# Second score matmul of the forgetting and stick-breaking heads over 128 rows, with zero rows in a low tile per head

## The chip, the cores and the metric

The kernel runs on one core of one Trainium2 chip. The metric is the device time of one execution in microseconds (us). Times of the kernel before come from three timed runs and from one further execution that the hardware profiler recorded. In the profile PE is TensorE (matmuls), PEld its weight loads, DVE is VectorE, ACT is ScalarE, POOL is GpSimd and SP is SyncE, which issues most DMAs. L65 is line 65 of the kernel.

## The reference

The program is a trunk of two layers on 512 tokens of width 1024. In each layer one input projection feeds three causal mixers of eight heads with 64 dimensions each; their outputs are projected, gated, added and projected again:

```python
h = rms_norm(x, g_norm) * (1.0 + scale) + shift
z = h @ w_in                                    # queries, keys, values, gates
y_fox = fox_attention(fq, fk, fv, log_f)        # softmax(q k^T / 8 + F_i - F_j), causal
y_dsa = dsa_attention(q_d, dk, dv, iq, ik, iw)  # one shared key head, top-k by indexer scores
y_sb = stick_breaking_attention(sq, sk, sv)     # sigmoid(z) * prod(1 - sigmoid(z)) of later keys
mixed = m_fox * (y_fox @ w_br_fox) + m_dsa * (y_dsa @ w_br_dsa) + m_sb * (y_sb @ w_br_sb)
x = x + gate * (mixed @ w_out)
```

The output is `rms_norm(x, g_final)` after the second layer. What matters here are the scores `q k^T` of the forgetting (fox) and the stick-breaking (sb) heads, 16 heads per layer, computed per block of 128 queries against all keys up to that block: 128, 256, 384 and 512 keys.

## The kernel before

**Precision by splitting.** Matmul operands are rounded to a short type, so each operand x is kept as a high part (`hi`, L116, a copy by ACT into the short type) and a low part (`lo`, L119, x minus high, by DVE). A projection adds three products, high by high, high by low and low by high (`mm3`): 24 matmuls for 8 chunks of 128 rows.

**Scores.** A head has 64 dimensions and the array contracts over 128 rows. So a head's query tile (`stack_q`, L440) holds the query's high part in one half of its rows and its low part in the other; for an even head the high part is in rows 0 to 63, for an odd one in rows 64 to 127. The key's high tile `kh` (`pair_k`, L766) holds the key's high part twice, in both halves. The first score matmul of a block, over 128 rows, so gives (query high + query low) by key high. The second adds query high by key low: it takes only the 64 rows in which the query's high part lies (`q[hr, c]`, where `hr(o)` is the half of head o) and the same rows of the key's low tile `kl`. One `kl` serves the two heads of a pair, one in each half. Both matmuls go into the same PSUM bank, with the same 128 query columns as weights (L637, L638 for fox; L656, L657 for sb).

The DSA heads have one key for all heads. Their `stack_k` (L447) makes a `kh` and a `kl` of 128 rows from a tile that holds the key twice, and both of their score matmuls contract over 128 rows (L641).

**What follows a score block.** Fox and DSA: DVE adds the bias and takes the row's minimum (L623), ACT exponentiates (L624). In a fox block POOL has first broadcast the forget row and masked it (L632, L634). Sb: ACT writes two sigmoids (L660, L661), POOL masks both (L662, L663), DVE does a running product (L665) and a multiplication (L666). Then PE transposes the probabilities, ACT and DVE split them (L117, L121), and PE multiplies them with the values.

**Buffers.** Tiles come from pools by tag. The tag `kh` has five buffers, `kl` three, `qst` (query tiles) six; in `project` (L808) the mixed activations reuse them, the first five chunks `kh`, the others `kl`. The four small PSUM banks `pt` hold scores and transposes.

**Order.** The order on PE and on SP is written out by hand when the program is built: one stream of projections (GEMMs), into which timed threads (heads, indexer, modulation) put their blocks. The clock of this order (`mm`, L63) counts the columns of each matmul at 2400 per us, whatever its rows. A head becomes startable 3.0 us of that clock after its pair's key projection (`pair`), heads start every 15 (fox), 13 (sb) and 14 us (DSA), and a small bank counts as held for 4.0 us. The order on ACT, DVE and POOL is chosen by the framework's planner from its own estimates; each engine then runs its queue in that order. The modulation of later layers (`ada`) runs on DVE beside all this, and so does, once the indexer's scores are complete, its top-k (L613, L614).

Of the kernel before, what the change touches and what calls it, by code (L numbers as in the profile page):

```python
# [12 lines left out]
F32 = mybir.dt.float32  # L13
F32R = mybir.dt.float32r
# [4 lines left out]
P = 128  # L19
D = 1024  # L20
S = 512
# [16 lines left out]
class Trunk:  # L38
# [12 lines left out]

# [1 line left out]
    def t(self, shape, dt, tag, bufs=1):  # L53
# [7 lines left out]

# [1 line left out]
    def mm(self, o, s, m, first, last):  # L63
# [26 lines left out]
    def bank(self, us):  # L90
        """Wait for one of the four small banks, to be held for about us."""
        if min(self.tfree) > self.now:
            yield lambda: min(self.tfree) <= self.now
        self.tfree[self.tfree.index(min(self.tfree))] = self.now + us
# [19 lines left out]

# [1 line left out]
    def hi(self, out, in_, scale=1.0):  # L116
# [35 lines left out]
    def gemm_b(self, ps, ws, n, tbs, ks=range(KC)):  # L152
        """h[tb] @ w for up to two token blocks: n <= 256 columns each, in one bank."""
        for i, tb in enumerate(tbs):
            sl = slice(tb * P, tb * P + P)
            o = ps[:, i * n:(i + 1) * n]
            for k in ks:
                wh, wl = ws[k // 4]
                hh, hl = self.hH[:, k, sl], self.hL[:, k, sl]
                self.mm(o, hh, wh[:, k % 4, :], k == 0 and i == 0, False)  # L160
                self.mm(o, hh, wl[:, k % 4, :], False, False)
                self.mm(o, hl, wh[:, k % 4, :], False, k == KC - 1)
                yield
# [33 lines left out]

# [1 line left out]
    def setup(self):  # L199
# [73 lines left out]

# [1 line left out]
    def ada_sum(self, acc, v, j, k, k0=0):  # L275
# [35 lines left out]
    def ada_first(self, b):  # L311
        """Columns 256b.. of scale and shift; the first rows of shift are left to the tensor engine."""
        n = PE_ROWS[b]
        tag = "tmp" if b % 2 else "fm"
        accs = [self.t([P, 256], F32, tag, 2) if part or n < 4 else None for part in range(2)]
        vs = []
        for j in range(KC // 2):
            for part in (1, 0):
                v = self.t([P, 2, 256], F32, *(("pt", 4) if b % 2 and not part else ("y", 8)))
                src = self.a["w_ada"][0, j * 256:(j + 1) * 256, part * D + b * 256:part * D + b * 256 + 256]  # L320
                self.nc.sync.dma_start(v, src.rearrange("(k p) n -> p k n", p=P))
                if not part and j < n:
                    vs.append(v)
                    continue
                for i in range(2):
                    self.ada_sum(accs[part], v, i, 2 * j + i, 0 if part else 2 * n)
        return accs, vs
# [22 lines left out]

# [1 line left out]
    def rstd(self, out, ssq, n):  # L352
# [47 lines left out]
    def rows(self, r, tag, tbs):  # L400
        """rstd of token blocks tbs along the free dimension, on every partition."""
        rb = self.ps(tag)
        for i, tb in enumerate(tbs):
            self.tp(rb[:, i * P:(i + 1) * P], r[:, tb:tb + 1].to_broadcast([P, P]))
        return rb
# [22 lines left out]

# [1 line left out]
    def rope(self, outs, x, cb, sb):  # L430
# [15 lines left out]

    def stack_k(self, src, tags=(("kh", 5), ("kl", 3))):  # L447
        pt = self.ps("t")
        for tb in range(NB):
            self.tp(pt[:, tb * P:(tb + 1) * P], src[:, tb, :])  # L450
        kh, kl = [self.t([P, S], F32R, *x) for x in tags]
        self.hi(kh, pt)
        self.lo(kl, pt, kh)
        return kh, kl

# [1 line left out]
    def small_raw(self, l, j):  # L457
# [86 lines left out]

# [1 line left out]
    def rope_bank(self, ps, tbs, qs, off, scale, key):  # L546
# [27 lines left out]

# [1 line left out]
    def indexer(self, l, iqs):  # L576
# [40 lines left out]

# [1 line left out]
    def softmax_block(self, ps, bias, n, b, den):  # L619
# [6 lines left out]

    def fox_block(self, h, b, q, kh, kl, hr, den):
        nc = self.nc
        n = (b + 1) * P
        part = 32 * (h % 4)  # L630
        fm = self.t([P, 512], F32, "fm", 2)
        nc.gpsimd.partition_broadcast(fm[:, :n], self.frow[h // 4][part:part + 1, :n])  # L632
        d = fm[:, b * P:n]
        nc.gpsimd.affine_select(d, d, [[-1, P]], ALU.is_ge, BIG, base=0, channel_multiplier=1)  # L634
        ps = self.ps("t")
        c = slice(b * P, n)
        self.mm(ps[:, :n], q[:, c], kh[:, :n], True, False)  # L637
        self.mm(ps[:, :n], q[hr, c], kl[hr, :n], False, True)  # L638
        return self.softmax_block(ps, fm[:, :n], n, b, den[:, b:b + 1])
# [10 lines left out]

    def sb_block(self, b, q, kh, kl, hr):
        nc = self.nc
        n = (b + 1) * P
        c = slice(b * P, n)
        ps = self.ps("t")
        self.mm(ps[:, :n], q[:, c], kh[:, :n], True, False)  # L656
        self.mm(ps[:, :n], q[hr, c], kl[hr, :n], False, True)  # L657
        u = self.t([P, 512], F32, "fm", 2)
        s = self.t([P, n], F32, f"pr{b}", 1 + (b != 1))
        nc.scalar.activation(u[:, :n], ps[:, :n], AF.Sigmoid, scale=-1.0)  # L660
        nc.scalar.activation(s, ps[:, :n], AF.Sigmoid)  # L661
        nc.gpsimd.affine_select(u[:, c], u[:, c], [[-1, P]], ALU.is_ge, 1.0, base=-1, channel_multiplier=1)  # L662
        nc.gpsimd.affine_select(s[:, c], s[:, c], [[-1, P]], ALU.is_ge, 0.0, base=-1, channel_multiplier=1)  # L663
        rev = u[:, :n][:, ::-1]
        nc.vector.tensor_tensor_scan(rev, rev, rev, 1.0, ALU.mult, ALU.bypass)  # L665
        nc.vector.tensor_tensor(s[:, :n - 1], s[:, :n - 1], u[:, 1:n], ALU.mult)  # L666
        return s
# [78 lines left out]

# [1 line left out]
    def values(self, l, col, u, out, key):  # L748
# [17 lines left out]
    def pair_k(self, ps, k):  # L766
        kl = self.t([P, S], F32R, "kl", 3)
        for o in range(2):
            a = slice(64 * o, 64 * o + 64)
            b = slice(64 - 64 * o, 128 - 64 * o)  # L770
            kh = self.t([P, S], F32R, "kh", 5)
            self.hi(kh[a, :], ps[a, :])
            self.hi(kh[b, :], ps[a, :])
            self.lo(kl[a, :], ps[a, :], kh[a, :])
            k.append(kh)
        k.append(kl)

    def pair(self, l, kind, cols, p, scale, st):
        """Query and key stacks and gate of heads 2p and 2p + 1."""
        q, k = st[p] = ([], [])  # L780
        yield from self.a_gemm(l, cols[0] + p * P, lambda ps: self.pair_q(ps, scale, q))
        yield from self.a_gemm(l, cols[1] + p * P, lambda ps: self.pair_k(ps, k))
        self.mark((kind, l, "pair", p), 3.0)
# [24 lines left out]
    def project(self, l, gate, out, st):  # L808
        nc = self.nc
        last = l + 1 == DEPTH  # L810
        mH, mL = [], []
        for m in range(KC):
            mH.append(self.t([P, S], F32R, *(("kh", 5) if m < 5 else ("kl", 3))))
            mL.append(self.t([P, S], F32R, *(("qst", 6) if m < 6 else ("pt", 4))))
            self.hi(mH[m], self.mix[m])
            self.lo(mL[m], self.mix[m], mH[m])
# [61 lines left out]

# [1 line left out]
    def opening_first(self, xc, rb, mod, fox, h, sps, sms, post):  # L880
        """The opening of layer 0, on two chunks of h at a time, as scale and shift come."""
        whole = slice(0, S)
# [73 lines left out]
    def opening(self, l, fox, st, gs, xc, mod):  # L956
        """Small columns and the first pair, on the parts of h as they come."""
        q, k = st[0] = ([], [])
# [38 lines left out]
    def attention(self, l, L):  # L997
        """Starts the heads of the three branches at an even pace."""
        hr = lambda o: slice(64 * o, 64 * o + 64)
        self.av_busy = False  # L1000
        prev = None
        self.spawn(self.indexer(l, L["iq"]))
        for kind, scale, period in (("fox", -0.125, FOX_T), ("sb", 0.125, SB_T), ("dsa", -0.125, DSA_T)):
            st, gs, ys = L[kind]
            den = y = None
            for h in range(NH):
# [13 lines left out]
                if kind == "fox":  # L1020
                    block = lambda b, h=h, q=q, k=k, o=o, d=den[:, o, :]: self.fox_block(h, b, q, k[o], k[2], hr(o), d)
                elif kind == "sb":
                    block = lambda b, q=q, k=k, o=o: self.sb_block(b, q, k[o], k[2], hr(o))
                else:
                    block = lambda b, q=q, d=den[:, o, :]: self.dsa_block(b, q, d)
# [176 lines left out]
```

## Time and profile before

| | us |
|---|---|
| median of three runs | 1333.29 (1332.83 to 1336.71) |
| span of the profiled execution, first to last instruction | 1328.5 |
| median of the runs less the profiled span | 4.8 |
| PE busy | 1297.9 |
| PEld busy | 1086.6 |
| DVE busy | 972.8 |
| ACT busy | 667.6 |
| POOL busy | 136.1 |

The profiled execution's own time is known as its span; the 4.8 us are the difference to the runs' median. Matmuls are pipelined, so the durations of neighbours overlap: a 128x512 matmul is shown as some 0.39 us long while the next one starts 0.23 us after it. What a matmul costs PE is therefore read from start to start. The granted clock of TensorE was 0.993 over the whole span, and 1.00 in all stages used below. Moving operands are written as partitions x columns, and `64*128` is the part of the array that a matmul uses: 64 rows, 128 columns.

### The profile page before, as it was taken

The numbers are of one execution on the slowest core, as the hardware profiler recorded it, in microseconds if no ns is written. First come the engines' busy times: TensorE is split into PE (matmuls) and PEld (weight loads), VectorE is DVE, ScalarE is ACT, GpSimd is POOL, SyncE is SP. The second block draws the span as 40 slices with busy tenths as digits, with TensorE's granted clock in tenths as the row PEclk, the third lists the DMA queues.
The fourth block names the chain that finished last, engine by engine and source line by source line (L and its number), as shares of the span: only waits on it lengthen the run. The fifth ranks groups of instructions, "written<-read, shape, count | busy, mean of one in ns | idle before, by whom it ended". The sixth has DMA issues, their size and how long they took to land.

```text
span 1328.5 us, 19568 instructions
## 1 busy us (share of the span) xinstructions
PE 1297.9 (98%) x7121; PEld 1086.6 (82%) x7121; DVE 972.8 (73%) x1963; ACT 667.6 (50%) x1303; POOL 136.1 (10%) x311
## 2 busy tenths in 40 slices
PE   6999999999999999999999999999999999999997
PEld 6888777878778888887899987787877888888887
DVE  5788777789999768566567866678989975756553
ACT  4366555464545545453236665556544564554343
POOL 0002122212122000000000212121111100000000
PEclk7999999999999999999999999999999999999999
DMA  9453233332333333242533232223222222324231
GB/s 286 142 175 112 66 110 95 95 91 72 113 92 96 111 94 114 82 133 87 153 100 112 81 96 64 80 64 96 64 80 83 77 80 80 95 64 119 87 103 73
DMA packets 193457, 133.34 MB, mean 100 GB/s; under 512 B 9456, under 2 KB 188224, under 8 KB 193360
## 3 DMA queue, kind: packets, MB, share of 16 engines
q1 hardware_dynamic: 189872, 125.76, 33.1%
q10 hardware_dynamic: 3488, 6.33, 1.5%
q8 instruction: 56, 0.92, 0.3%
q14 instruction: 41, 0.34, 0.1%
HBM read 125.74 MB, written 6.29 MB: 99 GB/s over the span
## 4 chain that ended last, share of the span: by engine, by line
PE 88%; DVE 4%; DMA 4%; issue 2%; ACT 2%; POOL 0%; SPq 0%; DVEq 0%; POOLq 0%; ACTq 0%
PE pg L65 67%; PE pt L65 10%; PE pt L69 5%; PE pa L65 5%; DMA y<-in_w_ada_dram 2%; DVE wl L121 1%; DMA raw<-in_w_in_dram 1%; DMA vs<-in_x_dram 1%; DVE fm L665 0%; DMA raw<-in_w_ada_dram 0%; ACT wh L117 0%; DMA y<-in_w_kv_up_dram 0%; DVE m L613 0%; DVE pr L666 0%; DVE score L614 0%
## 5 line engine op out<-in xcount | busy, mean ns | idle before, releaser
L65 PE MATMUL pg<-hH,wh 128*128 128x512 f32 (+1 forms) x848 | 346.2, 408 | 0.3 <-ACT wh L117 0.3
L65 PE MATMUL pg<-hH,wl 128*128 128x512 f32 (+1 forms) x848 | 331.6, 391 | 0.8 <-DVE wl L121 0.8
L65 PE MATMUL pg<-hL,wh 128*128 128x512 f32 (+1 forms) x848 | 331.2, 391 | 0.0
L121 DVE TENSOR_TENSOR wl<-raw,wh 128x1024 fp32r<-128x1024 f32 (+1 forms) x178 | 217.4, 1222 | 84.3 <-ACT wh L117 81.5
L117 ACT ACTIVATE wh<-raw 128x1024 fp32r<-128x1024 f32 (+1 forms) x178 | 187.8, 1056 | 175.8 <-PE pg L65 113.0
L65 PEld LDWEIGHTS pg<-hH,wh 128*128 128x128 f32 x848 | 159.7, 188 | 37.4 <-issue 8.0
L65 PEld LDWEIGHTS pg<-hH,wl 128*128 128x128 f32 x848 | 159.4, 188 | 37.3 <-DVE wl L121 1.0
L65 PEld LDWEIGHTS pg<-hL,wh 128*128 128x128 f32 x848 | 160.4, 189 | 25.6
L117 ACT ACTIVATE pt<-pt 128x512 fp32r<-128x512 f32 x192 | 83.7, 436 | 109.9 <-PE pt L69 108.0
L65 PE MATMUL pg<-wh,hH 128*128 128x256 f32 x448 | 131.4, 293 | 0.0
L121 DVE TENSOR_TENSOR pt<-pt,pt 128x512 fp32r<-128x512 f32 x192 | 93.3, 486 | 45.7 <-ACT pt L117 44.2
L65 PE MATMUL pg<-wh,hL 128*128 128x256 f32 x448 | 126.5, 282 | 0.0
L65 PE MATMUL pg<-wl,hH 128*128 128x256 f32 x448 | 125.8, 281 | 0.0
L65 PE MATMUL pg<-y,wh 128*128 128x512 f32 x384 | 123.8, 403 | 0.4 <-DVE y L121 0.4
L624 ACT ACTIVATE pr<-pr,nm 128x128 f32<-128x128 f32 (+3 forms) x128 | 71.6, 559 | 80.5 <-DVE nm L623 80.1
L65 PEld LDWEIGHTS pg<-wh,hH 128*128 128x128 f32 x448 | 84.7, 189 | 5.3 <-issue 2.9
L69 PE MATMUL pt<-ident,pr 128*128 128x128 f32 x480 | 84.8, 274 | 1.8 <-DVE pr L666 1.8
L65 PEld LDWEIGHTS pg<-wl,hH 128*128 128x128 f32 x448 | 84.7, 189 | 0.7
L65 PEld LDWEIGHTS pg<-wh,hL 128*128 128x128 f32 x448 | 84.4, 188 | 0.0
L65 PEld LDWEIGHTS pg<-y,wh 128*128 128x128 f32 x384 | 69.0, 188 | 16.9 <-issue 2.3
L65 PE MATMUL pg<-y,wl 128*128 128x512 f32 x192 | 76.0, 396 | 0.0
L69 PEld LDWEIGHTS pt<-ident,pr 128*128 128x128 f32 x480 | 60.1, 141 | 17.3 <-DVE pr L666 2.5
(216 smaller groups left out, 2270.0 us busy)
## 6 DMA issues: line engine op xcount, KB each, us to landing
raw<-in_w_in_dram SPq DMA_DIRECT2D x134, 512.0 KB, 3.9
raw<-in_w_ada_dram SPq DMA_DIRECT2D x32, 512.0 KB, 3.6
raw<-in_w_out_dram SPq DMA_DIRECT2D x16, 512.0 KB, 4.0
y<-in_w_ada_dram SPq DMA_DIRECT2D x24, 256.0 KB, 4.9
raw<-in_w_br_fox_dram SPq DMA_DIRECT2D x8, 512.0 KB, 3.7
raw<-in_w_br_sb_dram SPq DMA_DIRECT2D x8, 512.0 KB, 4.9
raw<-in_w_br_dsa_dram SPq DMA_DIRECT2D x8, 512.0 KB
yf<-xd ACTq DMA_DIRECT2D x16, 256.0 KB, 3.4
```

Source lines behind the costliest of these rows:

```text
L65: self.nc.tensor.matmul(o, s, m, start=first, stop=last, skip_group_check=True)
L69: self.nc.tensor.transpose(o, i, self.ident[:n, :n])
L117: self.nc.scalar.activation(out, in_, AF.Copy, scale=scale)
L121: self.nc.vector.tensor_tensor(out, in_, hi.bitcast(F32), ALU.subtract)
L624: nc.scalar.activation(p, p, AF.Exp, bias=nm, scale=-1.0, accum_out=den)
```

## The change

The second score matmul of a fox or sb block takes all 128 rows of the query tile and of a low tile of its own head. That low tile has the key's low part in the rows where the query's high part lies, and zeros in the other 64 rows, written by a memset on POOL. So there is one `kl` per head instead of one per pair, and the tag `kl` has five buffers instead of three, in all three places that name it. The scratch memory that is kept for dynamic DMAs is set to 2048 bytes per partition. The rest of the diff removes comments and doc strings.

```diff
-    def stack_k(self, src, tags=(("kh", 5), ("kl", 3))):
+    def stack_k(self, src, tags=(("kh", 5), ("kl", 5))):
...
-    def fox_block(self, h, b, q, kh, kl, hr, den):
+    def fox_block(self, h, b, q, kh, kl, den):
...
         self.mm(ps[:, :n], q[:, c], kh[:, :n], True, False)
-        self.mm(ps[:, :n], q[hr, c], kl[hr, :n], False, True)
+        self.mm(ps[:, :n], q[:, c], kl[:, :n], False, True)
...
-    def sb_block(self, b, q, kh, kl, hr):
+    def sb_block(self, b, q, kh, kl):
...
         self.mm(ps[:, :n], q[:, c], kh[:, :n], True, False)
-        self.mm(ps[:, :n], q[hr, c], kl[hr, :n], False, True)
+        self.mm(ps[:, :n], q[:, c], kl[:, :n], False, True)
...
     def pair_k(self, ps, k):
-        kl = self.t([P, S], F32R, "kl", 3)
         for o in range(2):
             a = slice(64 * o, 64 * o + 64)
             b = slice(64 - 64 * o, 128 - 64 * o)
             kh = self.t([P, S], F32R, "kh", 5)
+            kl = self.t([P, S], F32R, "kl", 5)
+            self.nc.gpsimd.memset(kl[b, :].bitcast(F32), 0.0)
             self.hi(kh[a, :], ps[a, :])
             self.hi(kh[b, :], ps[a, :])
             self.lo(kl[a, :], ps[a, :], kh[a, :])
-            k.append(kh)
-        k.append(kl)
+            k.append((kh, kl))
...
-            mH.append(self.t([P, S], F32R, *(("kh", 5) if m < 5 else ("kl", 3))))
+            mH.append(self.t([P, S], F32R, *(("kh", 5) if m < 5 else ("kl", 5))))
...
-    nc = _bacc.Bacc("TRN2", target_bir_lowering=False, num_devices=1)
+    nc = _bacc.Bacc("TRN2", target_bir_lowering=False, num_devices=1, dynamic_dma_scratch_size=2048)
```

In `attention` the two `block` lines pass `*k[o]`, the head's own pair of tiles, in place of `k[o]`, `k[2]` and `hr(o)`.

## Rows read from the trace of the kernel before

**Rows 1.** The page's first part: engine, busy us, share of the span, instructions.

```profile
PE 1297.9 (98%) x7121; PEld 1086.6 (82%) x7121; DVE 972.8 (73%) x1963; ACT 667.6 (50%) x1303; POOL 136.1 (10%) x311
```

**Rows 2.** The page's fourth part, the chain of work that ended last, as shares of the span by engine.

```profile
PE 88%; DVE 4%; DMA 4%; issue 2%; ACT 2%; POOL 0%; SPq 0%; DVEq 0%; POOLq 0%; ACTq 0%
```

**Rows 3.** Busy time by stage. Columns: stretch (us from the span's start), its length, then busy us and number of instructions of PE, PEld, DVE, ACT and POOL, the granted clock of TensorE, the share of the DMA engines, GB/s. The fourth row is from a table of 40 equal slices.

```profile
299.00:432.00 133.00, 131.51 (x692) 105.61 (x691) 126.69 (x240) 65.21 (x128) 26.16 (x55) 1.00 0.32 93
...
731.00:897.00 166.00, 166.00 (x910) 136.82 (x909) 117.50 (x262) 91.44 (x190) 34.87 (x65) 1.00 0.28 77
...
930.00:1063.00 133.00, 132.06 (x690) 106.25 (x689) 121.81 (x223) 65.88 (x130) 19.88 (x52) 1.00 0.27 76
...
398.50:431.70 33.20, 33.20 (x201) 27.73 (x200) 32.32 (x65) 17.75 (x37) 7.75 (x16) 1.00 0.34 96
```

**Rows 4.** Waits of PE from 299 to 432 us: who waited for whom, us in total, times, longest.

```profile
PE pt L69 <- DVE pr L666: 1.1, 1, 1.1
PE pa L65 <- DVE pt L121: 0.4, 1, 0.4
```

**Rows 5.** Busy time by stretch for the instructions that write or read tiles named `kl`: stretch, length, busy us and number of PE, PEld, DVE and ACT, granted clock, DMA. The PE instructions in these stretches are the 64-row score matmuls.

```profile
299.00:432.00 133.00, 10.75 (x26) 4.75 (x26) 3.44 (x5) 0.00 (x0) 1.00 0.32 93
930.00:1063.00 133.00, 10.51 (x26) 4.75 (x26) 4.11 (x6) 0.00 (x0) 1.00 0.27 76
98.00:299.00 201.00, 15.37 (x38) 6.84 (x38) 6.85 (x10) 0.00 (x0) 1.00 0.34 97
731.00:930.00 199.00, 14.73 (x36) 6.58 (x36) 6.17 (x9) 0.00 (x0) 1.00 0.30 80
1063.00:1078.00 15.00, 0.93 (x2) 0.36 (x2) 0.00 (x0) 0.00 (x0) 1.00 0.38 106
```

**Rows 6.** The timeline of PE around eight score blocks: start us, duration us, engine, line, operation, out<-in, rows*columns of the array, moving operand. Four blocks of fox or sb heads (low part with 64 rows) and four of DSA heads (128 rows); in order 512, 512, 384, 384, 256, 256, 128 and 128 columns, the fox or sb block first.

```profile
901.34 0.40 PE L65 MATMUL pt<-kh,qst 128*128 128x512 f32 x1
901.66 0.49 PE L65 MATMUL pt<-kl,qst 64*128 64x512 f32 x1
902.08 0.50 PE L65 MATMUL pg<-hH,wh 128*128 128x512 f32 x1
902.43 0.40 PE L65 MATMUL pg<-hL,wh 128*128 128x512 f32 x1
...
450.00 0.40 PE L65 MATMUL pt<-kh,qst 128*128 128x512 f32 x1
450.23 0.40 PE L65 MATMUL pt<-kl,qst 128*128 128x512 f32 x1
450.47 0.39 PE L65 MATMUL pg<-hH,wh 128*128 128x512 f32 x1
450.70 0.40 PE L65 MATMUL pg<-hL,wh 128*128 128x512 f32 x1
...
301.00 0.33 PE L65 MATMUL pt<-kh,qst 128*128 128x384 f32 x1
...
301.96 0.39 PE L65 MATMUL pg<-hL,wh 128*128 128x512 f32 x1
...
447.92 0.33 PE L65 MATMUL pt<-kh,qst 128*128 128x384 f32 x1
...
448.49 0.39 PE L65 MATMUL pg<-hL,wh 128*128 128x512 f32 x1
...
126.65 0.28 PE L65 MATMUL pt<-kh,qst 128*128 128x256 f32 x1
...
127.51 0.39 PE L65 MATMUL pg<-hL,wh 128*128 128x512 f32 x1
...
445.59 0.28 PE L65 MATMUL pt<-kh,qst 128*128 128x256 f32 x1
...
446.05 0.40 PE L65 MATMUL pg<-hL,wh 128*128 128x512 f32 x1
...
1001.44 0.22 PE L65 MATMUL pt<-kh,qst 128*128 128x128 f32 x1
...
1002.18 0.39 PE L65 MATMUL pg<-hL,wh 128*128 128x512 f32 x1
...
441.56 0.22 PE L65 MATMUL pt<-kh,qst 128*128 128x128 f32 x1
...
442.01 0.40 PE L65 MATMUL pg<-hL,wh 128*128 128x512 f32 x1
```

**Rows 7.** The group of the weight loads of the 64-row matmuls: count | busy us, mean ns of one | idle us of the load port before them, and what ended most of it.

```profile
L65 PEld LDWEIGHTS pt<-kl,qst 64*128 64x128 f32 x128 | 23.4, 183 | 31.1 <-issue 27.9 <-DVE kl L121 0.6 <-DVE mod L290 0.2
```

**Rows 8.** POOL: a memset of 128 columns (count | busy us, mean ns | idle before); the selects of L663 with their shortest, median and longest duration in ns; and two rows of the waits over the whole span (us in total, times, longest).

```profile
L208 POOL MEMSET pen<- 128x128 f32 x1 | 0.2, 206 | 0.0
...
L663 POOL TENSOR_SCALAR_AFFINE_SELECT pr<-pr x64: 289/295/2077, 278.3 to 1068.0; 128x128 f32<-128x128 f32 x64
...
POOL fm L662 <- ACT fm L660: 279.1, 64, 20.2
...
DVE fm L665 <- POOL fm L662: 9.7, 13, 2.4
```

More of the change, by code (lines that the diff above doesn't have):

```diff
@@ L997, in attention @@
     def attention(self, l, L):
-        hr = lambda o: slice(64 * o, 64 * o + 64)
         self.av_busy = False
@@ L1020, in attention @@
                 if kind == "fox":
-                    block = lambda b, h=h, q=q, k=k, o=o, d=den[:, o, :]: self.fox_block(h, b, q, k[o], k[2], hr(o), d)
+                    block = lambda b, h=h, q=q, k=k[o], d=den[:, o, :]: self.fox_block(h, b, q, *k, d)
                 elif kind == "sb":
-                    block = lambda b, q=q, k=k, o=o: self.sb_block(b, q, k[o], k[2], hr(o))
+                    block = lambda b, q=q, k=k[o]: self.sb_block(b, q, *k)
                 else:
```

## The prediction

> **What bounds the kernel now.** I read the page's busy shares first [rows 1]: TensorE (PE) is busy 1297.9 of the 1328.5 us span, 98%, VectorE (DVE) 73%, GpSimd (POOL) 10%. The chain of work that ended last [rows 2] is PE for 88%. So PE's instruction stream sets the time nearly everywhere: what shortens the distance from one matmul's start to the next shortens the kernel, as long as the engines that feed PE keep up. The table of stages [rows 3] shows where that is in doubt. From 299 to 432 us and from 930 to 1063 us, the stick-breaking heads of the two layers, DVE is busy 126.69 and 121.81 of 133 us, beside a PE that is busy 131.51 and 132.06. There two engines are nearly full at once, and what PE gains it can keep only up to DVE's idle time. The waits of PE in the first of these stages [rows 4] are two, 1.1 and 0.4 us, both on DVE: today DVE is just in time.
>
> Then the blocks that the change touches. A score block is two matmuls with the same query tile as weights: with the key's high part (128 rows), then with its low part (64 rows). The same tile query over five stretches [rows 5] counts the 64-row ones: 38, 26, 36, 26 and 2, in all 128 (2 layers, 16 heads, 4 blocks), so 32 of each width, 128, 256, 384 and 512 columns. A mean duration doesn't tell what one costs, since durations overlap; starts in the timeline do. The DSA heads run the same pair of widths with a full 128-row low part, in the same kernel and at the same granted clock, so the price after the change is already in the trace [rows 6].
>
> From the start of the high matmul to the start of the second matmul behind the pair, both followers being 128x512 of a projection:
> - 512 columns: 901.34 to 902.43 with 64 rows, 1.09 us; 450.00 to 450.70 with 128 rows, 0.70 us. Difference 0.39.
> - 384 columns: 301.00 to 301.96, 0.96; 447.92 to 448.49, 0.57. Difference 0.39.
> - 256 columns: 126.65 to 127.51, 0.86; 445.59 to 446.05, 0.46. Difference 0.40.
> - 128 columns: 1001.44 to 1002.18, 0.74; 441.56 to 442.01, 0.45. Difference 0.29.
>
> In the full sequences of 512 columns the loss has three places: the 64-row matmul starts 0.32 us after the high one instead of 0.23, the follower 0.42 after it instead of 0.24, and the matmul after that 0.35 later instead of 0.23. The weight-load row says why: before the 128 loads of 64 rows the load port stood idle 31.1 us, 27.9 of it "issue", waiting for nothing that the profile shows [rows 7]. With full rows a load is done beside the matmul before it; where the row count changes, it is not, on the way in and on the way out.
>
> The Trainium skill (TensorEngine Tiling (Array Packing), Key Properties) says that changing the tiling mode drains TensorE. The trace agrees, with those 0.24 us per load. The same page (Theoretical Speedup) promises up to 2x for contractions of at most 64 rows, by running separate tiles of the array at once. By that rule the change would give up a speed-up instead of removing a cost; the trace shows none of it, since no 64-row matmul here stands beside another one.
>
> **The change part by part.**
> 1. The second score matmul takes 128 rows: 128 times, none added or moved. Sum of the four differences 0.39 + 0.39 + 0.40 + 0.29 = 1.47 us, times 32 = 47.0 us, 0.367 per block. This is the whole gain if nothing else becomes late.
> 2. What DVE leaves of it. Outside the two full stages stand 38 + 36 + 2 = 76 blocks: 76 x 0.367 = 27.9 us, taken whole, since their slack is large (DVE there is busy 117.50 of 166 us from 731 to 897 us [rows 3]). From 299 to 432 us the 26 blocks are worth 9.5 us, but DVE is idle only 133 - 126.69 = 6.3. DVE's fullest slice today runs at 32.32 of 33.20, 97.3% [rows 3]; at that share its 126.69 us take 130.2 (gain 2.8), at 99% they take 128.0 (gain 5.0). I take 4. From 930 to 1063 us the 26 blocks are again worth 9.5; DVE's 121.81 us take 125.2 at 97.3% (gain 7.8) and less than PE's demand at 99% (all 9.5). I take 8. Bounds for the two together: 0 (DVE's queue already as late as it can be) and 19.
> 3. Memset of 64x512 on POOL, one per head: 32. Not in the trace. POOL's memset of 128 columns takes 0.206 us [rows 8]; four times that is 0.82 us, 26 us in all, and that I take. Bound above: a POOL select that took 2.08 us instead of 0.30 [rows 8], so 67 us. POOL idles 90%, and the first score matmul of a pair is planned 3 us or more behind the key's projection, which covers both figures. The second score matmul of a head now also waits for this memset. On POOL it stands behind broadcasts and selects of earlier blocks, whose matmuls are ahead in PE's order as well; behind the memset on POOL stand the next blocks' selects, and DVE's scans wait for those (9.7 us in all today [rows 8]). Between 0 and 3 us per pair; I take 0, because almost all of POOL's waiting is for work that has not been issued.
> 4. Two low tiles per pair instead of one, in five buffers instead of three: they are allocated and freed together with the high tiles, which have five and are needed by the same matmuls, so no new wait for a buffer. ACT and DVE instructions of the key stacks keep their number and shape. Cost 0.
> 5. The smaller scratch of dynamic DMAs: every issue on the page comes from SP's and ACT's queue, none from POOL. Cost 0.
> 6. PE's order and the DMA order are written out by a clock that counts columns alone, so they stay. The order on ACT, DVE and POOL is chosen anew with 32 instructions more; from -2 to +2 us, I take 0. For scattered new waits, now that PE comes sooner to everything, I take 1 us.
>
> Sum: 27.9 + 4 + 8 - 1 = 38.9 us off the span, 1328.5 to 1289.6. The median of the timed runs lies 4.8 us above the profiled span (1333.29); with that kept, 1294.
>
> **Rivals.**
> - *Everything is kept.* DVE's queue is packed by PE's pace and closes up fully, and shorter score blocks also reach it sooner. For it: the second full stage has 11 us of DVE idle time. Against: the first has 6.3. 47.0 off: 1286.
> - *The full stages give nothing, and waits eat a part of the rest.* With DVE at its end in both stages, and its lag carried on to the merges behind them, 27.9 less some 5 for waits on split weights: 23 off, 1310. For it: PE's two waits on DVE in rows 4. Against: in the second stage DVE has idle time enough.
> - *Padding does not help.* If the slow start belonged to the low tile or to the shared weights and not to the row count, the pair would cost the same: 1333. Against: rows 6 show the pair with 128 rows, also after shared weights, at full pace.
> - *Slower, by the memset.* One tile is now written by POOL and by DVE. If DVE's subtraction into the lower rows is held until POOL's memset is done, and the memset sits behind a select that waits for ACT (279.1 us over 64 waits, 4.4 each [rows 8]), DVE stands still in the stages where it is full. The price is 4.4 us for each of the 16 pairs, 70 us; with 47 gained, 23 slower: 1356. It decides from 47 / 16 = 2.9 us per pair on. Against it: the memset needs no projection and can run well before the subtraction, and the two write different rows.
>
> **How the numbers follow.** The forecast (1289 to 1299) 0.53, everything kept 0.21, the half gain (1300 to 1315) 0.19, padding without effect 0.03, slower by the memset 0.04. The range that holds 8 in 10 is 1284 to 1309: it takes in the full gain and most of the half. What a measurement can tell from no change is 0.3%, 4 us. Faster 0.93, same 0.03, slower 0.04.
>
> **What would show it.** Right: no 64-row matmul left, the score pairs at the spacings of the DSA heads (0.70 us and 0.45 us for 512 and 128 columns), the weight loads of the low part without idle time; the stages without full DVE shorter by 0.37 us per block; in the first full stage a DVE at 98% and PE with some 5 us of waits on it. Wrong: waits of PE on a POOL memset, of DVE's low-part subtraction on POOL, or score pairs that keep their old spacing. A first full stage shorter by all of 9.5 us would show that I held DVE too slow.

## The result and the profile after

The changed kernel takes 1302.06 us (median, 1299.83 to 1305.84), the kernel before in the same series 1334.49 us. The ratio is 0.9762, 95% interval 0.974 to 0.9784: 32 us less, where 39 were forecast and 47 stood to be had. A second series of the changed kernel gave 1298.8 us beside 1332.08, ratio 0.9747 (0.9726 to 0.9768). Three executions that took over 1900 us, two of the first experiment below and one of the kernel before in its series, are left out of all medians and ratios.

The price per block came out as read from the DSA heads. Two blocks of the changed kernel on PE (start us, duration us, engine, line, operation), 512 and 128 columns:

```profile
134.53 0.39 PE L65 MATMUL pt<-kh,qst 128*128 128x512 f32 x1
134.76 0.39 PE L65 MATMUL pt<-kl,qst 128*128 128x512 f32 x1
135.00 0.39 PE L65 MATMUL pg<-hH,wh 128*128 128x512 f32 x1
135.22 0.39 PE L65 MATMUL pg<-hL,wh 128*128 128x512 f32 x1
...
155.65 0.22 PE L65 MATMUL pt<-kh,qst 128*128 128x128 f32 x1
155.70 0.28 PE L65 MATMUL pt<-kl,qst 128*128 128x128 f32 x1
155.81 0.45 PE L65 MATMUL pg<-hH,wh 128*128 128x512 f32 x1
156.10 0.40 PE L65 MATMUL pg<-hL,wh 128*128 128x512 f32 x1
```

From the high matmul to the second follower it is 0.69 and 0.45 us, against 1.09 and 0.74 before [rows 6]. The weight loads show the same from the other side. All 192 of the low part now have 128 rows (the 64 of the DSA heads are among them), and the 31.1 us of idle load port [rows 7] have shrunk to 6.0, none of it "issue". The group line below gives count | busy us, mean ns | idle before; under it stand the new memsets (shortest, median, longest ns):

```profile
L65 PEld LDWEIGHTS pt<-kl,qst 128*128 128x128 f32 x192 | 36.2, 189 | 6.0 <-DVE kl L121 0.3
```

```profile
L772 POOL MEMSET kl<- x32: 517/520/526, 3.2 to 959.5; 64x512 f32 x32
```

PE executes the same 7121 matmuls in the same order in both kernels, so the start of the n-th matmul can be set against the start of the n-th. That gives a table of stages that end at the same matmul; it is worked out from the two timelines, and the last column from a second profile of the changed kernel.

| stage (us in the kernel before) | 64-row blocks | before | after | gain | second profile |
|---|---|---|---|---|---|
| opening, to 99.8 | 1 | 99.8 | 103.3 | -3.5 | 103.8 |
| fox, layer 0, to 266 | 31 | 166.3 | 154.9 | 11.4 | 154.9 |
| first sb blocks, to 299 | 6 | 33.2 | 31.7 | 1.5 | 31.7 |
| sb, layer 0, to 432 | 26 | 132.7 | 132.0 | 0.7 | 131.9 |
| rest of layer 0, to 631 | 0 | 199.0 | 199.1 | -0.1 | 199.0 |
| project and opening of layer 1, to 731 | 0 | 99.8 | 100.9 | -1.1 | 98.5 |
| fox, layer 1, to 897 | 30 | 166.1 | 156.6 | 9.5 | 155.2 |
| to 930 | 6 | 33.3 | 31.1 | 2.2 | 31.1 |
| sb, layer 1, to 1063 | 26 | 132.7 | 127.0 | 5.7 | 126.6 |
| last sb blocks, to 1096 | 2 | 33.3 | 32.6 | 0.7 | 32.6 |
| rest of layer 1 | 0 | 232.3 | 232.4 | -0.1 | 232.3 |

Three things are to be read from it. In the fox stage of layer 0 a block gives 11.4 / 31 = 0.37 us, to the last digit what was forecast. In the sb stage of layer 0 the same 26 blocks give 0.03 us each, and in layer 1 0.22. And the two openings, which hold one of these blocks in all, cost 4.6 us.

Busy time of the changed kernel in the two sb stages (stretch, length, busy us and count of PE, PEld, DVE, ACT, POOL, granted clock, DMA), answering to the first and third row of rows 3, and PE's waits in the first of them, answering to rows 4:

```profile
289.60:421.70 132.10, 125.56 (x691) 106.68 (x691) 126.52 (x241) 65.10 (x128) 28.14 (x58) 0.99 0.34 96
909.40:1036.60 127.20, 123.45 (x689) 105.99 (x688) 120.65 (x223) 65.52 (x130) 20.45 (x55) 1.00 0.28 79
```

```profile
PE pa L65 <- DVE pt L121: 4.2, 6, 1.9
PE pt L69 <- DVE pr L666: 2.2, 2, 2.0
```

DVE's work in the first stage is what it was (126.52 us against 126.69), the stage is nearly as long as it was, and 4.9 us of what PE gained stand there as waits on DVE, 6.4 us in place of 1.5. Behind the longest wait of the second row, which ends at 368.61 us, the granted clock of TensorE falls as well (columns as above):

```profile
365.00:370.00 5.00, 2.77 (x14) 1.99 (x13) 5.00 (x9) 2.09 (x3) 0.00 (x0) 1.00 0.16 50
370.00:375.00 5.00, 5.00 (x19) 4.04 (x18) 4.41 (x8) 1.40 (x4) 1.13 (x2) 0.66 0.44 123
```

A mean of 0.66 over 5 us means that PE worked for 3.4 us at the lower of TensorE's two levels, 1.2 instead of 2.4 GHz, and what it does there takes 1.7 us longer. The second profile of the changed kernel has the same fall at the same place. Some 2 us of the 9.5 that the 26 blocks are worth are named by no row.

The share that is DVE's own time in the chain of work that ended last has grown from 4% [rows 2] to 11%:

```profile
PE 79%; DVE 11%; DMA 4%; issue 3%; ACT 2%; SPq 0%; POOL 0%; DVEq 0%; POOLq 0%; ACTq 0%
```

### The profile page after: what moved, and what is told of

It reads as the page before. It is cut to its first block, busy times and chain, and to the rows that moved or that the text cites. A ratio compares the mean times of both kernels' runs of the same rounds, so it can differ in the third digit from the quotient of the medians.

```text
span 1301.7 us, 19621 instructions
## 1 busy us (share of the span) xinstructions
PE 1263.4 (97%) x7121; PEld 1093.0 (84%) x7121; DVE 968.8 (74%) x1963; ACT 664.8 (51%) x1303; POOL 152.4 (12%) x343
## 4 chain that ended last, share of the span: by engine, by line
PE 79%; DVE 11%; DMA 4%; issue 3%; ACT 2%; SPq 0%; POOL 0%; DVEq 0%; POOLq 0%; ACTq 0%
PE pg L65 60%; PE pt L65 9%; PE pa L65 5%; PE pt L69 5%; DVE wl L121 2%; DVE fm L665 2%; DMA raw<-in_w_in_dram 2%; DVE m L613 1%; DVE score L614 1%; DVE pr L666 1%; DVE ada L280 1%; ACT wh L117 1%; DMA vs<-in_x_dram 1%; DVE pt L121 0%; DVE mix L804 0%
## 5 line engine op out<-in xcount | busy, mean ns | idle before, releaser
L65 PE MATMUL pg<-hH,wh 128*128 128x512 f32 (+1 forms) x848 | 340.7, 402 | 0.3 <-ACT wh L117 0.3
L65 PE MATMUL pa<-pt,vs 128*128 128x512 f32 (+3 forms) x256 | 70.4, 351 | 6.5 <-DVE pt L121 6.4
```

Of the source, the lines that this page charges most:

```text
L65: self.nc.tensor.matmul(o, s, m, start=first, stop=last, skip_group_check=True)
```

## Experiments

The times below are medians, the ratios those to the kernel before in the same series; the stages are cut as in the table, at the n-th matmul of PE's order.

### Everything but the rows

```diff
-        self.mm(ps[:, :n], q[:, c], kl[:, :n], False, True)
+        hr = slice(64 * (h % 2), 64 * (h % 2) + 64)
+        self.mm(ps[:, :n], q[hr, c], kl[hr, :n], False, True)
```

(The same in the sb block.)

> The changed kernel with its low tile per head, its memsets, its buffers and its scratch size, but with the second score matmul over 64 rows again, as before. Theory (the whole gain comes from the row count of the matmul; memset, buffers and scratch cost nothing): the time of the kernel before, 1334 us, within 4. Rival (memsets, the new order on ACT, DVE and POOL, or the memory layout cost the 7 us that are missing from the forecast gain of 39): 1341.

Measured: 1332.4 us, ratio 0.9991 (0.9973 to 1.001). The stages have their lengths of before (166.3, 33.2 and 132.7 us in layer 0). So the memsets, the second low tile and the scratch size cost nothing that can be measured, and the gain is the matmul's. (The order on ACT, DVE and POOL, which was expected to be chosen anew, is the same in the traces of all three kernels, but for the 32 memsets.) Its opening took 104.9 us, longer than any other here, with memsets and without full rows.

### Fox alone, sb alone

The changed kernel, with the edit above in one of the two kinds of head.

> The changed kernel with full rows in the fox heads alone; the sb heads contract over 64 rows. Theory (a block is worth 0.37 us where DVE has idle time, and next to nothing while DVE is full): the 64 fox blocks lie outside the full stages, so 64 x 0.36 = 23 us less than before, 1311. Rival (each block keeps the same share of its worth, 32 / 47, wherever it stands): 16 less, 1318.

> The changed kernel with full rows in the sb heads alone; the fox heads contract over 64 rows. Theory (DVE is at its end in the sb stages): the sb blocks give the 6 us that the stages of the changed kernel show for them (0.6 in layer 0, 5.7 in layer 1) and some 3 for those that start before DVE is full, 9 in all, 1325. Rival (the same share everywhere): 16 less, 1318.

Measured: fox alone 1308.46 us, ratio 0.9815 (0.9789 to 0.984), 25 us less; sb alone 1321.13 us, ratio 0.9915 (0.9888 to 0.9942), 11 to 12 us less. The same share everywhere would be 16 and 16, and lies outside both intervals. With fox alone the fox stages shrink by 11.4 and 10.9 us and the sb stages stay (132.5 and 132.6). With sb alone the sb stage of layer 0 gives 2.3 us, where with both it gives 0.7. It was forecast at 0.6 and so missed. PE waits there about as long as in the changed kernel (6.7 us against 6.4), and the longest wait on L667, which is L666 of the changed kernel, is 2.0 us in both, but here the clock does not fall behind it. The stage of this run (columns as above):

```profile
301.10:431.50 130.40, 123.67 (x690) 105.39 (x689) 126.45 (x240) 65.35 (x129) 25.61 (x58) 1.00 0.33 98
```

It is 1.6 us shorter than in the changed kernel, about what the clock took there, and DVE fills 97.0% of it. The next run, with full rows in both kinds of head, has the same 2.0 us wait, no fall of the clock, and 130.2 us in this stage. Why the clock falls in one run and not in the other is open. In layer 1 the stage gives 6.1.

### The cost put where it was not

```diff
-        self.mm(ps[:, :n], st, kl[:, :n], False, True)
+        hr = slice(64 * o, 64 * o + 64)
+        self.mm(ps[:, :n], q[hr, b * P:n], kl[hr, :n], False, True)
```

> The changed kernel with the DSA heads' second score matmul over the 64 rows of the query's high part; this leaves out the product of query low part and key low part. It puts the suspected cost where it was not, 64 blocks in a stage where DVE is idle a third of the time. Theory (leaving and entering the 64-row form costs 0.37 us per block): 64 x 0.37 = 23 us more than the changed kernel, 1325. Rival (the cost belonged to the pair tiles of fox and sb, their shared low tile or their place among the projections): no change, 1302.

Measured: 1320.87 us, 19 us more than the changed kernel in its first series and 22 more than in its second. The stages that hold the DSA blocks grew from 199.1 to 210.2 us in layer 0 and, the last two of the table together, from 265.0 to 276.1 in layer 1: 22.2 us for 64 blocks, 0.35 each. The timeline of this run has the old spacing, now in a DSA head (compare 450.00 in rows 6):

```profile
454.13 0.40 PE L65 MATMUL pt<-kh,qst 128*128 128x512 f32 x1
454.46 0.50 PE L65 MATMUL pt<-kl,qst 64*128 64x512 f32 x1
454.89 0.50 PE L65 MATMUL pg<-hH,wh 128*128 128x512 f32 x1
455.23 0.40 PE L65 MATMUL pg<-hL,wh 128*128 128x512 f32 x1
```

1.10 us instead of 0.70. So it is the row count, and not the tiles or the kind of head; DVE has idle time here, and nearly the whole price appears.

### Is it the change of form, or each 64-row matmul?

The kernel before, with

```diff
-        self.mm(ps[:, :n], q[hr, c], kl[hr, :n], False, True)
+        self.mm(ps[:, :n // 2], q[hr, c], kl[hr, :n // 2], False, True)
+        self.mm(ps[:, n // 2:n], q[hr, c], kl[hr, n // 2:n], False, True)
```

in the fox heads.

> The kernel before with each 64-row score matmul of the fox heads split into two of half the columns, same weights and rows. Theory (the cost lies in going from 128 rows to 64 and back, once each per block): the second half adds at most the 0.1 us of a short matmul, 64 blocks, 0 to 6 us more, 1334 to 1340. Rival (each 64-row matmul starts some 0.2 us late, whatever stands before it): 13 us more, 1347.

Measured: 1339.85 us, ratio 1.0057 (1.0042 to 1.0072), 8 us more by the medians, between the two. The stages decide: fox in layer 0 went from 166.3 to 167.5, in layer 1 from 166.1 to 167.3, so 2.4 us for the 61 added matmuls that lie there, 0.04 us each and not 0.2. The rest of the 8 us lies in the two openings (103.0 and 103.4 us), which hold one fox block; in the second of them the granted clock was 0.50 from 693.4 to 700.2 us, which costs 3.4 us. In the timeline the pair of halves is one row:

```profile
136.68 0.40 PE L65 MATMUL pt<-kh,qst 128*128 128x512 f32 x1
137.01 0.50 PE L65 MATMUL pt<-kl,qst 64*128 64x256 f32 x2
137.44 0.50 PE L65 MATMUL pg<-hH,wh 128*128 128x512 f32 x1
137.77 0.39 PE L65 MATMUL pg<-hL,wh 128*128 128x512 f32 x1
```

From 136.68 to 137.77 it is 1.09 us, as with one 64-row matmul [rows 6]. The late start is paid on the way in (0.33 us for a matmul that otherwise takes 0.23) and on the way out, once per block. The Trainium skill (TensorEngine Tiling (Array Packing), Key Properties) says that a change of the tiling mode drains TensorE and a change of tile within it does not; these runs agree as to the mode, and the other half was not tried, since both halves used the same rows.

### Less work for DVE in the sb stage

```diff
-            for _ in range(16):
-                m8 = self.t([P, 8], F32, "m8", 2)
-                self.pin(nc.vector.max(m8, s))
-                nc.vector.match_replace(s, m8, s, SENT)
+            for i in range(16):
+                if i % 2 == 0:
+                    m8 = self.t([P, 8], F32, "m8", 2)
+                    self.pin(nc.vector.max(m8, s))
+                    nc.vector.match_replace(s, m8, s, SENT)
                 yield TOPK_GAP
```

> The changed kernel with every second round of the top-k left out (8 of 16 rounds per query block, so half of the keys are selected), PE's order untouched. This takes some 28 us of DVE work from each layer, about a third of it in the stage where DVE is full. Theory (DVE's end is what took the gain of the sb stages): PE keeps 8 us more in layer 0 and 3 to 4 in layer 1, 1291. Rival (the sb stages lose the gain to something else, POOL's selects, ACT or the small banks): 1302, or 1300 with PE's few present waits on DVE gone.

> The kernel before with every second round of the top-k left out, the control of the run above. Theory (before, PE itself was the bound, with 2 us of waits on DVE in the sb stages): 1334 to 1332. If DVE was the bound of these stages already before, as much as after: 1323, the same 11 us less as in the changed kernel.

Measured: in the changed kernel 1293.3 us, ratio 0.9718 (0.9699 to 0.9737), 9 less than in its first series and 5.5 less than in its second; in the kernel before 1333.14 us, ratio 1.0013 (1.0 to 1.0026). So the same work is worth nothing in the time of the kernel before and something in that of the changed one, which was the point of the pair: PE was the bound, and DVE became one. But by stage it is not as expected. In the changed kernel the sb stage of layer 1 went from 127.0 to 122.7 us, the 4 us forecast; that of layer 0 only from 132.0 to 129.5, and the 33 us before it took 1.1 us longer. 3.5 of the 9 us are a quick opening (99.8 us). In the kernel before the sb stage of layer 1 went from 132.7 to 131.5 us, and that of layer 0 grew from 132.7 to 134.7, with one wait on DVE of 2.5 us and 3.4 us at half the clock behind it. With less top-k the other work on DVE also stands in another order in places, so the pair does not change the amount of work alone. The windows of layer 0 show what is left (columns as above; this run; the first is a long stretch around the other two):

```profile
289.60:421.70 132.10, 126.08 (x705) 108.44 (x704) 113.88 (x205) 64.18 (x127) 24.29 (x56) 0.99 0.31 91
...
360.00:365.00 5.00, 0.24 (x3) 0.01 (x1) 5.00 (x9) 0.00 (x0) 0.00 (x0) 1.00 0.07 9
365.00:370.00 5.00, 4.32 (x14) 3.57 (x15) 2.96 (x4) 1.93 (x4) 0.00 (x0) 0.66 0.29 99
```

and the one wait of PE in that stretch, from the timeline, with what released it:

```profile
365.69 0.45 PE L69 MATMUL pt<-ident,pr 128*128 128x128 f32 x1 [5.44 <-DVE pr L667]
```

(L667 is L666 of the changed kernel.) For 5 us DVE worked without a gap while PE did next to nothing, although over the long stretch DVE had 18 us of idle time (113.88 busy of 132.10). The chain of waits names the order of DVE's queue just then:

```profile
359.55 0.69 DVE mix L805
360.24 0.60 DVE m L614
360.84 1.12 DVE fm L666
361.96 0.06 DVE yf L738
...
362.46 1.22 DVE wl L121
363.68 0.66 DVE score L615 x2
364.34 0.59 DVE mix L805
364.94 0.61 DVE pr L667
...
365.69 0.45 PE pt L69
```

Between the product scan of a block (L666) and the multiplication that PE waits for (L667) stand a gate product, a weight split, a top-k step and a merge, work that PE was not waiting for then. So it is DVE, but not its sum alone: its queue is in order, and a block's last step stands behind whatever was placed ahead of it. After the wait the granted clock of the next 5 us was 0.66, a mean over TensorE's two levels, so this wait of PE cost 1.7 us more than its length.

### Modulation moved out of the sb stage

```diff
-                yield gap
+                self.pieces = getattr(self, "pieces", 0) + 1
+                yield self.has("qk", 0, "sb", NH - 1) if self.pieces == 12 else gap
...
-            yield from self.ada(ll, part, out, 400.0 / (8 * len(parts)))
+            yield from self.ada(ll, part, out, 10.0 if l == 0 else 400.0 / (8 * len(parts)))
```

> The changed kernel with the modulation sums of layer 0 moved: 12 of the 24 pieces at the start at a shorter gap (10 us), a pause until the last sb score block, then the other 12. All is computed. Each piece is about 2 us of DVE; some 8 leave the full stage of layer 0. Theory (DVE's end): that stage gets its gain back, 7 to 9 us less than the changed kernel, 1294. Rival (another cause, or the pieces only press on DVE elsewhere): 1302 or a little more.

> The same move of the modulation sums in the kernel before. Theory (PE was the bound there): 1334, or 1333 with its present waits of 1.5 us on DVE gone. Rival (the move is worth as much without the change): 1326.

> As the run that moved the modulation sums of layer 0 in the changed kernel, but with a gap of 12.5 us instead of 10, so that the pieces press less on DVE before and behind the sb stage; that run won 5.5 us in the sb stage of layer 0 and lost 1.9 and 3.5 us in the stages around it. Theory (DVE's end in the sb stage is what took the gain): the 5.5 stay and the losses shrink to 1 or 2 in all, 4 us less than the changed kernel. Rival (wherever the pieces are put they cost PE the same): no difference from the changed kernel.

> The changed kernel once more, beside the others on the same chip. 1302, and in its profile the same stages as in the first, but for the opening, which differs from run to run.

Measured: in the changed kernel 1299.33 us, with the wider gap 1298.11; the changed kernel in the same series as the latter 1298.8, where 1302 was expected of it. In the kernel before 1334.45 us, ratio 1.0017 (0.9999 to 1.0035). By the medians nothing, so in the time the rival was right; by stage the mechanism is plain. The sb stage of layer 0 fell from 132.0 to 126.7 us (wider gap: 126.5), while in the kernel before the same move left it at 132.7. The edit also moves the modulation's small matmuls on PE, those of one column, from stage to stage (12 of them in this stage become 4), so the n-th matmul is not quite the same one here. Between the same score matmuls the stage fell by 7.2 us in the changed kernel and by 1.9 in the kernel before; the difference is 5.3 either way. With some 7.5 us less DVE work (119.04 against 126.52) PE got these 5.3 us back, 1.7 of them because the clock does not fall:

```profile
291.30:418.00 126.70, 123.63 (x691) 106.03 (x689) 119.04 (x217) 64.64 (x129) 24.82 (x58) 1.00 0.24 71
```

What it won there it lost around it: the fox stage of layer 0 grew from 154.9 to 156.8 (wider: 156.0), the rest of layer 0 from 199.1 to 202.6 (wider: 202.9), so the hope of smaller losses fell. The chain of the first of these runs shows one of the places:

```profile
466.92 0.50 DVE ada L280
...
467.44 0.48 DVE ada L280
467.92 0.03 DVE pr L624
467.95 4.73 DMA raw<-in_w_in_dram
...
472.70 1.07 ACT wh L117
...
473.79 1.23 DVE wl L121
```

A piece of modulation does not only take DVE's time, it occupies one of the two `raw` buffers through which the projections' weights come. While DVE sums it, the load that waits for this buffer can't start, and that load, its split and PE behind it come late.

### The last product of sb on POOL

```diff
-        nc.vector.tensor_tensor(s[:, :n - 1], s[:, :n - 1], u[:, 1:n], ALU.mult)
+        nc.gpsimd.tensor_tensor(s[:, :n - 1], s[:, :n - 1], u[:, 1:n], ALU.mult)
```

> The changed kernel with the last product of each sb block on POOL instead of DVE. It takes 0.49 us of DVE from each of 64 sb blocks, some 15 us from each full stage, and adds more than that to POOL, which is busy 28 of 132 us there. Theory (DVE's end): the sb stages get 5 to 8 us back in layer 0 and 3 in layer 1, 1293. Rival (POOL is slower than DVE and the transposes now wait for it, in order behind the next block's selects): 1302 to 1315.

Measured: 1309.15 us, ratio 0.982 (0.9796 to 0.9844), 10 us more than the changed kernel in the same series; the rival's time. From 266 to 432 us the run took 167.7 us against 163.7. The product of 511 columns takes POOL 1.27 us, and PE waits for it:

```profile
L666 POOL TENSOR_TENSOR pr<-pr,fm 128x511 f32<-128x511 f32 x16 | 20.3, 1270 | 24.2 <-DVE fm L665 24.0
```

```profile
PE pa L65 <- DVE pt L121: 5.7, 4, 3.4
PE pt L69 <- POOL pr L666: 4.6, 3, 3.0
```

(The second fence holds PE's waits from 260 to 427 us of this run.) The rival's reason, that the product stands behind the selects in POOL's order, is not what the trace has: before the 511-column products POOL sat idle 24.2 us, nearly all for DVE's scan, and before the one of the 3.0 us wait it was idle for 3.30 us. The scan comes late, and the product behind it is slower on POOL. Taking work off DVE does not help if the block's own path gets longer by it.

## Why the prediction was right, and where not

The direction, the range (1284 to 1309) and the mechanism held. The first series, 1302.06, lies among the times that I had given to the half gain (0.19), 3 us above those of my forecast (1289 to 1299); the second, 1298.8, lies at their upper end. Term by term:

- *128 blocks at 0.367 us, 47.0 in all.* Right. 0.37 in the fox stage of layer 0, 0.36 with the second profile in layer 1 (10.9 / 30), 0.35 when the DSA heads were given the old form. In the first profile the fox stage of layer 1 gave 1.4 us less, and there the clock stood at half from 721.5 to 724.9 us, behind a wait of 2.74 us on DVE. Reading the price from the same operation elsewhere in the kernel, and from start to start, was sound.
- *Outside the full stages 27.9.* Nearly right: 11.4 + 1.5 + 9.5 + 2.2 + 0.7 = 25.3 in the first profile, 26.7 in the second. The six blocks just before the sb stage of layer 0 gave 1.5 us where their widths promise 2.2; one wait of PE on DVE, 0.33 us, stands there, and the rest was not traced.
- *The sb stages 4 + 8.* Mis-sized, and the term in which the prediction erred most: 0.7 + 5.7 in the first profile, 0.8 + 6.1 in the second. Two things are in it. I let DVE fill to between 97.3% and 99%, above all to the share of its fullest 33 us. Over a whole stage it reached 97.0% in layer 0 where the clock did not fall (sb alone; 126.45 of 130.40) and 94.9% in layer 1 (120.65 of 127.20). With 97.0% the working for layer 0 would have given 126.69 / 0.970 = 130.6, a gain of 2.4 instead of 4. The other 1.7 us of layer 0 is the clock that fell behind a wait on DVE, for which the sum had no term. The waits that I named as the sign came (6.4 us for some 5); DVE at 98% did not.
- *Memset 0.82 us, hidden.* It takes 0.52, and no wait of PE or of DVE names it. The rival of the memset is out: without full rows, memsets and all, the time is that of before.
- *Buffers, scratch, order: 0.* Right, by the same run; the order did not change at all.
- *1328.5 to 1289.6, and 4.8 around the span.* The span came to 1301.7. Of the 12.1 us between, 5.6 are the sb stages, 4.6 the two openings, 2.6 the blocks outside the full stages, and 0.3 the stages without such blocks and rounding; 1.0 goes off again, which I had set aside for new waits. The openings are no effect of the change. The first took 99.8 to 104.9 us in the profiles of this study, the second 98.2 to 103.4, and kernels with full rows and with 64 rows lie at both ends (99.8 with full rows and half the top-k, 104.9 with 64 rows). The execution that was profiled before was among the quickest there. The changed kernel's own time in its profiled execution was 1303.39, 1.7 us around its span, and the executions of the kernel before on record show the same 1.7 (1335.01 and 1333.3); so of the 4.8 us that I kept about 1.7 lay around the span, and 3 were the distance of a quick execution from the median.

What makes the first opening longer is in good part the clock. From 40 to 50 us (columns as above), first the kernel before, then the changed one:

```profile
40.00:50.00 10.00, 9.38 (x64) 8.49 (x65) 9.20 (x23) 2.82 (x4) 0.00 (x0) 1.00 0.75 243
40.00:50.00 10.00, 10.00 (x43) 9.20 (x41) 6.84 (x15) 1.38 (x2) 0.00 (x0) 0.54 0.72 226
```

Over the first 100 us the granted clock was 0.93 before and 0.88 after, 5 us of full clock. It was 0.88 with 64 rows and memsets too, in the opening of 104.9 us.

The rival "the full stages give nothing, and waits eat a part of the rest" (1310) came closer for layer 0 than the forecast did. "Everything is kept" fell with rows that I had read: two waits of PE on DVE [rows 4] were a sign that DVE had little slack there, and I counted most of its idle time as slack all the same. What is still open is why the clock falls in one execution and not in another at the same place of the code, in the openings and behind a wait of 2 us; no run was made for it.

## What to carry to other kernels

If a kernel holds the same operation in two forms, compare them from start to start in its own timeline before building anything; here that gave the price to within 0.02 us. A matmul over half the rows among full ones costs the way in and the way out, so half the contraction can cost more than all of it. A gain on the bounding engine is kept only where the second engine has slack, and the slack of an in-order queue is not its idle time: look at how long the engine behind it already waits, and don't take the share of its fullest slice as its limit. Over a whole stage DVE reached 95 to 97% here.

## What was not expected of the hardware

- The 64-row form costs the same whether one matmul is issued in it or two of half the width (1.09 us from the high matmul to the second follower, 512 columns): the price lies in changing the row count.
- A wait of PE can cost more than its length: after 5.44 us of waiting the granted clock averaged 0.66 over the next 5 us. After a wait of 2.0 us it fell so in both profiles of the changed kernel and stayed at 1.00 in two of its variants.
- A POOL product of 511 columns takes 1.27 us, while the same on DVE was 0.68 (10.9 us for 16 in the kernel before); the 32 memsets of 512 columns on POOL take 0.52 us with a spread of 9 ns, while POOL's selects range from 0.29 to 2.08 us [rows 8].
